# A two-layer hybrid decoder step: decay moved onto the keys of a chunked state scan, longer pauses, own buffers for small results, and another model for the scheduler

## The chip, the core and the metric

The kernel runs on one core of a Trainium2 chip. Its engines work side by side, each through its own queue of instructions in order: TensorE (PE, with its weight loads as PEld), VectorE (DVE), ScalarE (ACT), GpSimd (POOL) and SyncE (SP), which here issues transfers. The metric is the device time of one execution in microseconds (us). What is compared is the median of several executions.

## The reference

Two layers of a decoder take one step for a prompt of 512 tokens and 8 samples of 4 tokens each, 544 token columns in all. Weights are shared, states are per sample. The model width is 1024, in 32-bit floats. Cut to what matters here, one layer is:

```python
h = rmsnorm(x, p['norm1_g']) * (1 + mod[:, 1]) + mod[:, 0]
z = h @ p['w_in']
# four mixers on column ranges of z: pooling (yA), retention (yB), short convolution (yC), RWKV-7 (yD)
proj = jnp.einsum('btnc,ncd->btnd', branches, p['w_br'])
mixed = jnp.sum(gates * proj, axis=2) @ p['w_out']
x = x + mod[:, 2] * mixed
h2 = rmsnorm(x, p['norm2_g']) * (1 + mod[:, 4]) + mod[:, 3]
up, n_ffn = causal_dwconv(h2 @ p['w_up'], st_ffn, p['ffn_w'])
x = x + mod[:, 5] * (act @ p['w_down'])

def rwkv7_scan(r, w, k, v, a_vec, b_vec, S0):      # S: value x key, per head (4 heads of 64)
    def step(S, inp):
        rt, wt, kt, vt, at, bt = inp
        S = (S * wt[:, :, None, :]
             + jnp.einsum('bhij,bhj->bhi', S, at)[..., None] * bt[:, :, None, :]
             + vt[..., :, None] * kt[..., None, :])
        return S, jnp.einsum('bhij,bhj->bhi', S, rt)
```

The decay w is a vector over the key index, for each token. Retention (yB) has a fixed decay per head and a state that is carried from one 128-token chunk to the next. The result of RWKV-7 is normalised per head, gets a bonus term and is gated.

## The kernel before, in words

**The weight stream.** All large products have the tokens as moving columns, in two halves of 272, and a 128x128 piece of a weight matrix as the stationary operand. Each weight is split into a high and a low part: the high part is a cast on ScalarE (L113, `whi`), the low part a subtraction on VectorE (L114, `wlo`; GpSimd does it for two units at the start). Activations are split in the same way (L394 and L395). A product is then three matmuls, L133 to L135: high by high, high by low, low by high. There are 13248 of them, and `nmm` counts them as they are written. Weights come in units of 128x1024 (0.5 MB), loaded by SyncE some units ahead. Results go to one of three PSUM buffers `pd`.

**Side work.** The mixers, the adaptive scale and shift (`ada`) and the normalisations are generators. After each three stream matmuls `slot()` looks which generators are due and writes their next piece into the program. A generator ends a piece with `yield n`: it is due again after n more stream matmuls. So a pause is a length in stream matmuls, in multiples of three as things fall. The order of TensorE's instructions is the order in which this code writes them (`manual_schedule`). The order on VectorE, ScalarE, GpSimd and SyncE is chosen by the framework's scheduler, which simulates the program by a model of costs, and every wait between engines is put in by the framework.

**RWKV-7.** `rwkv` works through the prompt in 16 chunks of 32 tokens; a seventeenth stands for the samples. First `products(T)` makes, for four chunks at a time, keys and values that are scaled by the accumulated decays (`bkv`, L481; the left-hand side is written at L473 and L475), and `dec`, the whole decay of each chunk. TensorE transposes the keys (L500, result `psB`, copied to `BK`) and multiplies them with the left-hand side (L507, `psA`). Both have the accumulated decay divided out up to the chunk's end, so the state has to be multiplied by `dec` after each chunk. Then the scan runs, chunk by chunk: the matmuls of L653 (`psG`), copies of it to `gs` on ScalarE and VectorE (L615), the matmul L620 with the solved triangular system, copies of that into Z (L624), L673 (`psP`, what the chunk adds to the state) and L677 (output `pY`). Then the state is updated: `Pt = psP + Pn` (L685), two products of `Pt` with `dec` that go into Z for the next chunk (L691), and `Pn = Pt * dec` on GpSimd (L692). The pauses inside a chunk are `D_G` (behind L653), `D_S` (behind L620) and `D_P` (at the end). After the scan come the per-head normalisation (L383 sums on TensorE, Ln and Exp on ScalarE in L388 and L391, L771 to L775 on VectorE) and `yD`.

**Retention** runs per pair of heads. Transposes and scores are at L791 and L798; in the second piece are the chunk states (L819, summed into `Sb` by L825 and L827 on VectorE) and a copy for the samples (`vks`); in the third the outputs (L839 and, with `Sb`, L844). Its rope products wait for a transfer that exchanges rows (L1218), then GpSimd multiplies (L1220).

**Residual.** After the output projection, each block of 128 channels is added to x. For the second half of the tokens `residual` reads the PSUM buffer twice, for the prompt columns (L346) and for the 32 sample columns (L350, whose gates differ per sample), and adds the second to x in L353. L309 makes the next normalised activations from x.

**Buffers.** Most intermediate tiles, large or small, are taken in turn from one ring of ten buffers of 128x562 (`ZR`).

## Time and profile before

| | |
|---|---|
| median of 3 runs | 1978.6 us (1977.38 to 1979.33) |
| the profiled execution | 1977.9 us, span 1976.1 us, mean granted clock 0.990 |
| TensorE busy | 1908.5 us, 97% of the span |
| VectorE, ScalarE, GpSimd busy | 1111.4, 831.2, 315.7 us |
| PE idle, by the busy time | 67.6 us |
| first matmul of the weight stream | 30.85 us |
| HBM read | 213.33 MB, 113 GB/s over the span |

A row of the profile names line, engine, operation, and output and inputs by the program's names. In a timeline row, the first number is the start and the second the duration (us), and a bracket at its end gives the idle time of the engine before it with what released it. In a row of the table of groups, the count is followed by the total busy time, the mean in ns, and the idle time before them. `pd` and `pm` are PSUM tiles, `zr` tiles of the ring, `t` tiles of several kinds.

### The profile page before, as it was taken

How to read it: one execution, taken by the hardware profiler on the slowest of the kernel's cores; microseconds unless marked ns; L12 is line 12 of the kernel's file. 1: busy time of each engine (PE TensorE's matmuls, PEld its weight loads, DVE VectorE, ACT ScalarE, POOL GpSimd, SP SyncE). 2: the span in 40 equal slices, each digit the busy share in tenths (PEclk: the TensorE clock that was granted, in tenths of full speed). 3: DMA queues.
4: the chain of work that ended last, by engine and by line, in shares of the span. 5: the costliest groups of instructions: out<-in, count | busy, mean ns of one | idle time of the engine just before them, and what ended most of it. 6: DMA issues, size and time to landing. Idle time of an engine off the chain costs nothing.

```text
span 1976.1 us, 39220 instructions
## 1 busy us (share of the span) xinstructions
PE 1908.5 (97%) x16188; PEld 1829.6 (93%) x16188; DVE 1111.4 (56%) x2267; ACT 831.2 (42%) x1581; POOL 315.7 (16%) x627
## 2 busy tenths in 40 slices
PE   5999999999999999999999999999999999999997
PEld 4989888899999998899989899889999999999997
DVE  5466654643565653455673667556335765455565
ACT  4642332452445531435455433326424555243542
POOL 2120123213001210112201201232210012011210
PEclk8999999999999999999999999999999999999998
DMA  7323434423342257622332132124224222222231
GB/s 311 98 87 112 139 117 149 141 82 95 125 148 104 91 205 291 234 86 86 120 130 66 57 106 68 65 95 127 76 85 163 72 80 93 86 86 86 90 101 46
DMA packets 75555, 227.16 MB, mean 115 GB/s; under 512 B 20208, under 2 KB 23072, under 8 KB 73584
## 3 DMA queue, kind: packets, MB, share of 16 engines
q1 hardware_dynamic: 69872, 210.43, 31.9%
q0 software_dynamic: 3536, 11.53, 1.7%
q10 hardware_dynamic: 1968, 2.69, 0.5%
q8 instruction: 127, 2.08, 0.4%
q14 instruction: 52, 0.43, 0.1%
HBM read 213.33 MB, written 9.06 MB: 113 GB/s over the span
## 4 chain that ended last, share of the span: by engine, by line
PE 90%; DVE 5%; ACT 2%; DMA 1%; issue 1%; DVEq 0%; ACTq 0%
PE pd L133 27%; PE pd L135 26%; PE pd L134 26%; PE pm L236 2%; DVE wlo L114 1%; PE pm L673 1%; ACT whi L113 1%; DMA raw<-in_wst 1%; PE pm L500 1%; PE pm L677 1%; PE pm L653 0%; DMA t<-in_wada 0%; PE pm L507 0%; PE pm L620 0%; PE pm L383 0%
## 5 line engine op out<-in xcount | busy, mean ns | idle before, releaser
L133 PE MATMUL pd<-t,whi 128*128 128x272 f32 x4104 | 1207.3, 294 | 7.5 <-DVE zr L350 3.6
L135 PE MATMUL pd<-t,wlo 128*128 128x272 f32 x4104 | 1187.5, 289 | 0.0
L134 PE MATMUL pd<-t,whi 128*128 128x272 f32 x4104 | 1181.8, 288 | 0.1
L133 PEld LDWEIGHTS pd<-t,whi 128*128 128x128 f32 x4104 | 773.9, 189 | 39.9 <-issue 26.4
L134 PEld LDWEIGHTS pd<-t,whi 128*128 128x128 f32 x4104 | 775.7, 189 | 1.3 <-DVE t L395 0.3
L135 PEld LDWEIGHTS pd<-t,wlo 128*128 128x128 f32 x4104 | 774.3, 189 | 0.0
L114 DVE TENSOR_TENSOR wlo<-raw,whi 128x1024 fp32r<-128x1024 f32 x256 | 316.9, 1238 | 301.7 <-ACT whi L113 301.4
L113 ACT CAST whi<-raw 128x1024 fp32r<-128x1024 f32 x258 | 270.5, 1049 | 433.4 <-PE pd L134 419.6
L1276 POOL COPY off<-zr 128x18 f32<-128x18 f32 x88 | 76.2, 866 | 558.8 <-ACT zr L1274 558.8
L346 DVE SCALAR_TENSOR_TENSOR t<-pd,mod,t 128x272 f32<-128x272 f32 (+1 forms) x160 | 76.9, 481 | 112.5 <-PE pd L135 111.6
L1274 ACT COPY zr<-pd 128x272 f32<-128x272 f32 (+2 forms) x264 | 72.7, 311 | 78.4 <-PE pd L135 78.4
L1129 ACT ACTIVATE zr<-pd 128x272 f32<-128x272 f32 x128 | 50.3, 395 | 110.3 <-PE pd L135 106.2
L1111 DVE TENSOR_TENSOR zr<-pd,zr 128x272 f32<-128x272 f32 x96 | 41.1, 437 | 98.8 <-PE pd L135 98.1
L1113 POOL TENSOR_TENSOR t<-t,zr 128x272 f32<-128x272 f32 x64 | 71.3, 1133 | 112.5 <-DVE zr L1111 112.4
L1040 DVE SCALAR_TENSOR_TENSOR zr<-zr,par,zr 128x560 f32<-128x560 f32 x92 | 73.4, 800 | 10.0 <-ACT zr L1039 9.9
L1041 DVE SCALAR_TENSOR_TENSOR zr<-zr,par,zr 128x560 f32<-128x560 f32 x92 | 73.4, 801 | 2.8
L1039 ACT ACTIVATE zr<-zr,par 128x560 f32<-128x560 f32 x92 | 70.2, 765 | 6.8
L394 ACT CAST t<-zr 128x544 fp32r<-128x544 f32 (+1 forms) x96 | 49.5, 530 | 53.4 <-DVE zr L1287 53.0
L395 DVE TENSOR_TENSOR t<-zr,t 128x544 fp32r<-128x544 f32 (+1 forms) x96 | 54.5, 580 | 30.7 <-ACT t L394 30.4
L276 ACT ACTIVATE zr<-t 128x272 f32<-128x272 f32 (+1 forms) x72 | 32.2, 455 | 82.8 <-DVE t L346 54.6
L133 PE MATMUL pd<-t,t 128*128 128x272 f32 x224 | 64.8, 289 | 0.2
L134 PE MATMUL pd<-t,t 128*128 128x272 f32 x224 | 64.5, 288 | 0.0
(283 smaller groups left out, 1770.1 us busy)
## 6 DMA issues: line engine op xcount, KB each, us to landing
raw<-in_wst SPq DMA_DIRECT2D x276, 512.0 KB, 3.4
t<-in_wada SPq DMA_DIRECT2D x32, 1024.0 KB, 9.5
raw<-in_wada SPq DMA_DIRECT2D x24, 512.0 KB, 3.4
zr<-in_rope POOLq DMA_DIRECT2D x16, 272.0 KB, 3.6
t<-in_wada SPq DMA_DIRECT2D x8, 512.0 KB, 6.1
t<-in_xT SPq DMA_DIRECT2D x4, 544.0 KB, 6.1
zr<-zr ACTq DMA_DIRECT2D x32, 68.0 KB, 2.9
t<-in_xT SPq DMA_DIRECT2D x2, 1088.0 KB, 7.1
```

Of the source, the lines that this page charges most:

```text
L113: S.copy(hi, raw)
L114: (G if (l, u) in ((0, 1), (0, 2)) else V).tensor_tensor(out=lo, in0=raw, in1=hi, op=SUB)
L133: PE.matmul(ps, lhsT=a, rhs=xh, start=first, stop=False)
L134: PE.matmul(ps, lhsT=a, rhs=xl, start=False, stop=False)
L135: PE.matmul(ps, lhsT=b, rhs=xh, start=False, stop=last)
L346: V.scalar_tensor_tensor(out=x[:, c0:c0 + npc], in0=ps[:, :npc], scalar=gate[:, m, 0:1], in1=x[:, c0:c0 + npc], op0=MUL, op1=ADD)
L1039: S.activation(cv, u[:, 0:560], AF.Copy, scale=wcol(0))
L1040: V.scalar_tensor_tensor(out=cv, in0=u[:, 1:561], scalar=wcol(1), in1=cv, op0=MUL, op1=ADD)
L1041: V.scalar_tensor_tensor(out=cv, in0=u[:, 2:562], scalar=wcol(2), in1=cv, op0=MUL, op1=ADD)
L1113: (V if last else G).tensor_tensor(out=a[:, c0:c1], in0=a[:, c0:c1], in1=gs, op=ADD)
L1274: pad_evac(lambda o, i, sl: S.copy(o, i), u, ps, half, 2)
L1276: G.tensor_copy(off[:, 22 * s + j], u[:, 512:562].rearrange("p (x t) -> p x t", t=2)[:, 0:25:3, :])
```

## The change

Four things are changed.

1. The pauses: `D_G`, `D_S` and `D_P` go from 12, 12, 18 to 16, 16, 20, and the two pauses around the products from 48 and 44 to 60 and 56. Because pieces are written at multiples of three, the pause behind L653 goes from 12 to 18 stream matmuls, and so does the one behind L620; a whole chunk goes from 42 to 57, a step of the products from 45 to 57.
2. The keys carry the decay of their chunk: `bkd = bkv * dec` is a new product on VectorE for the 16 prompt chunks (four per layer and four chunks each), and the transposes take `bkd`. `psP` then comes out already multiplied, so the state is `Z = psP + E` with `E = Z * dec` of the chunk after. The additions are done on VectorE straight from PSUM into Z; `E` is made on GpSimd, in two halves.
3. Four kinds of small results (32 or 128 columns) get a ring of their own of five buffers, `ZS`.
4. The scheduler of the other engines is given the timeline simulator as its model (`schedule_with_timeline_sim=True`).

```diff
-D_G, D_S, D_P = 12, 12, 18
+D_G, D_S, D_P = 16, 16, 20
...
+    zsp = ctx.enter_context(tc.tile_pool(name="zsp", bufs=5))
...
+    def ZS(n):
+        return zsp.tile([128, n], F32, tag="zs", name=nm("zs"))
...
             if half == 1:
-                t = ZR(32)
+                t = ZS(32)
...
-            return bkv
+
+            bkd = ZR(512)
+            bkdv = bkd[:, 0:4 * n].rearrange("p (q c x) -> p q c x", q=2, x=64)
+            if T < 4:
+                V.tensor_tensor(out=bkdv, in0=bkv.rearrange("p q c w t -> p q c (w t)"),
+                                in1=dec[:, :, 4 * T:4 * T + nch].unsqueeze(3).broadcast_to([128, 2, nch, 64]), op=MUL)
+            return bkv, bkdv if T < 4 else bkv.rearrange("p q c w t -> p q c (w t)")
 
         bkn = products(0)
-        yield 48, True
+        yield 60, True
...
-                        PE.matmul(psB[kv_rows(q), cc:cc + 64], lhsT=bkv[r, p, c].rearrange("r w t -> r (w t)"),
+                        PE.matmul(psB[kv_rows(q), cc:cc + 64], lhsT=bkd[r, p, c],
...
-                yield 44, True
+                yield 56, True
...
-            pP = psP[:, 0:128].rearrange("r (p i) -> r p i", p=2)
-            db = dec[:, :, ch:ch + 1].broadcast_to([128, 2, 64])
-            Pt = M["pool"].tile([128, 2, 64], F32, tag="pt", name=nm("pt"), bufs=2)
-            if Pn is None:
-                V.tensor_copy(Pt, pP)
-            else:
-                V.tensor_tensor(out=Pt, in0=pP, in1=Pn, op=ADD)
-            Pn = M["pool"].tile([128, 2, 64], F32, tag="pn", name=nm("pn"), bufs=2)
             if ch < 15:
                 Zt, cn = (Z, 1) if c % 2 == 0 else (Zn, 0)
+                E = M["pool"].tile([128, 2, 64], F32, tag="pt", name=nm("pt"), bufs=2)
                 for q in range(2):
                     r = par_rows(q)
-                    V.tensor_tensor(out=Zt[q][r, cn], in0=Pt[r], in1=db[r], op=MUL)
-            G.tensor_tensor(out=Pn, in0=Pt, in1=db, op=MUL)
+                    pP = psP[r, 0:128].rearrange("r (p i) -> r p i", p=2)
+                    if ch:
+                        V.tensor_tensor(out=Zt[q][r, cn], in0=pP, in1=Eo[r], op=ADD)
+                    else:
+                        V.tensor_copy(Zt[q][r, cn], pP)
+                    G.tensor_tensor(out=E[r], in0=Zt[q][r, cn], in1=dec[r, :, ch + 1:ch + 2].broadcast_to([64, 2, 64]), op=MUL)
+                Eo = E
...
-                g0 = ZR(128)
+                g0 = ZS(128)
...
-        sms_s = ZR(32)
+        sms_s = ZS(32)
-        vks = ZR(128)
+        vks = ZS(128)
...
-    with tile.TileContext(nc) as tc:
+    with tile.TileContext(nc, schedule_with_timeline_sim=True) as tc:
```

How this moves instructions is shown at three places. Lines of the changed kernel are 4 higher up to some L485, and 10 or 11 higher behind it.

The residual on VectorE, in the first layer's output projection at the second half of the tokens, before. L346 and L350 read the PSUM tile `pd`, L114 is a weight split, L290 and L309 belong to the next normalisation:

```order
L346 SCALAR_TENSOR_TENSOR t_845_6216<-pd_6489,mod_94,t_845_6216 128x240
L114 TENSOR_TENSOR wlo_6629<-raw_6626,whi_6628 128x1024
L290 RECIPROCAL zr_6516<-zr_6516 128x272
L346 SCALAR_TENSOR_TENSOR t_845_6216<-pd_6530,mod_94,t_845_6216 128x240
L309 TENSOR_TENSOR zr_6519<-t_845_6216,zr_6516 128x272
L350 TENSOR_TENSOR zr_6525<-pd_6489,mod_94 128x32
```

The same place now (L350 is the former L346, L354 the former L350, L118 the former L114, L294 the former L290):

```order
L350 SCALAR_TENSOR_TENSOR t_834_6211<-pd_6484,mod_97,t_834_6211 128x240
L354 TENSOR_TENSOR zs_6520<-pd_6484,mod_97 128x32
L357 TENSOR_TENSOR t_834_6211<-t_834_6211,zs_6520 128x32
L118 TENSOR_TENSOR wlo_6624<-raw_6621,whi_6623 128x1024
L294 RECIPROCAL zr_6511<-zr_6511 128x272
L350 SCALAR_TENSOR_TENSOR t_834_6211<-pd_6525,mod_97,t_834_6211 128x240
L354 TENSOR_TENSOR zs_6571<-pd_6525,mod_97 128x32
```

Both readers of a `pd` tile stand one behind the other now, where four instructions stood between them.

The first products of the first layer on VectorE, now, up to the new product (L491); L446 and L447 prepare the keys, L477 and L479 the left-hand side, L485 is the former L481, and L1051 the former L1040:

```order
L446 SCALAR_TENSOR_TENSOR t_121_999<-t_121_999 128x544
L447 TENSOR_TENSOR t_72_615<-t_72_615,zr_1153 128x544
L477 TENSOR_TENSOR t_149_1163<-t_121_999,zr_1169 64x2x4x31
L477 TENSOR_TENSOR t_150_1164<-t_121_999,zr_1169 64x2x4x31
L479 TENSOR_TENSOR t_150_1164<-t_73_616,zr_1169 64x2x4x32
L118 TENSOR_TENSOR wlo_1205<-raw_1202,whi_1204 128x1024
L485 TENSOR_TENSOR zr_1179<-t_121_999,zr_1169 128x4x32
L485 TENSOR_TENSOR zr_1179<-t_72_615,zr_1169 128x4x32
L491 TENSOR_TENSOR zr_1184<-zr_1179,dec_596 128x512
L118 TENSOR_TENSOR wlo_1269<-raw_1266,whi_1268 128x1024
L1051 SCALAR_TENSOR_TENSOR zr_1198<-zr_1135,par_91,zr_1198 128x560
```

A weight split (L118) now stands ahead of the last two products of the keys, and the sum L1051, which stood ahead of them, stands behind.

The end of RWKV-7 and the first retention pair of the first layer on VectorE, now. L782 to L786 are the former L771 to L775, L836 and L838 the former L825 and L827 (`Sb`), L842 the former L831:

```order
L782 TENSOR_TENSOR t_73_616<-t_73_616,zr_4661 128x544
L833 TENSOR_TENSOR zs_4784<-pm_4767,cst 64x32
L200 SCALAR_TENSOR_TENSOR scl_99<-mod_97,par_91 128x72
L842 TENSOR_TENSOR zr_4794<-zs_4786,cst 64x512
L783 TENSOR_SCALAR t_73_616<-t_73_616,par_91 128x544
L836 COPY t_632_4686<-pm_4775 128x64
L782 TENSOR_TENSOR t_73_616<-t_73_616,zr_4662 128x544
L785 TENSOR_TENSOR t_73_616<-t_73_616,t_121_999 128x544
L838 TENSOR_TENSOR t_632_4686<-pm_4775,t_632_4686 128x64
L783 TENSOR_SCALAR t_73_616<-t_73_616,par_91 128x544
L786 TENSOR_TENSOR t_73_616<-t_73_616,t_121_999 128x544
L838 TENSOR_TENSOR t_632_4686<-pm_4775,t_632_4686 128x64
```

Before, L771 to L775 were all done ahead of the first scores of retention, and L825 to L827 stood behind them with one weight split and L831 in between. Now the two are threaded.

## The prediction

> **What bounds the kernel now.** I read the page's busy times and its chain first.

> ```profile
> PE 1908.5 (97%) x16188; PEld 1829.6 (93%) x16188; DVE 1111.4 (56%) x2267; ACT 831.2 (42%) x1581; POOL 315.7 (16%) x627
> PE 90%; DVE 5%; ACT 2%; DMA 1%; issue 1%; DVEq 0%; ACTq 0%
> ```

> TensorE is busy for 1908.5 of the 1976.1 us span, and the change takes no matmul from it. So only its 67.6 us of idle time can move, and each term must name a stall of PE that shrinks, goes or is born. PE's table of waits lists them as total us, times, longest.

> ```profile
> PE pm L287 <- DVE zr L279: 14.9, 3, 12.4
> PE pm L620 <- DVE gs L615: 10.4, 10, 1.3
> PE pm L500 <- DVE zr L481: 8.4, 3, 4.0
> PE pd L133 <- DVE zr L350: 8.2, 6, 2.8
> PE pd L133 <- DVE zr L1111: 2.5, 2, 1.2
> ```

> The first is the start, before any work. The other four lie at places which the change rearranges: 29.5 us, 1.5% of the span, and that caps what it can win there. The unit of length is the weight stream of L133 to L135, since the hand-written PE order counts its pauses in those matmuls. From PE's timeline:

> ```profile
> 1015.17 0.37 PE L133 MATMUL pd<-t,whi 128*128 128x272 f32 x1 [2.82 <-DVE zr L350]
> 1015.38 0.29 PE L134 MATMUL pd<-t,whi 128*128 128x272 f32 x1
> ...
> 1017.40 0.29 PE L135 MATMUL pd<-t,wlo 128*128 128x272 f32 x1
> 1018.44 0.36 PE L133 MATMUL pd<-t,whi 128*128 128x272 f32 x1 [0.75 <-DVE zr L350]
> ```

> From 1015.38 to 1017.40 lie 16 steps: 0.126 us per matmul. A pause longer by 6 matmuls gives whoever is waited for 0.75 us, at no cost to PE, since the stream must run anyway.

> **Residual, the wait on L350.** Two of the six waits stand in the rows above. VectorE in the same window:

> ```profile
> 1012.59 0.46 DVE L346 SCALAR_TENSOR_TENSOR t<-pd,mod,t 128x240 f32<-128x240 f32 x1
> 1012.97 0.43 DVE L309 TENSOR_TENSOR zr<-t,zr 128x272 f32<-128x272 f32 x1
> 1013.35 1.23 DVE L114 TENSOR_TENSOR wlo<-raw,whi 128x1024 fp32r<-128x1024 f32 x1
> 1014.49 0.43 DVE L309 TENSOR_TENSOR zr<-t,zr 128x272 f32<-128x272 f32 x1
> 1014.84 0.18 DVE L350 TENSOR_TENSOR zr<-pd,mod 128x32 f32<-128x32 f32 x1
> ```

> L346 and L350 both read one PSUM buffer; PE needs it back. L350 takes 0.18 us and needs nothing but that buffer and the gate, yet VectorE does two L309 and a weight split in between: L350 ends at 15.02, 1.9 us after L346 could hand over (12.59 + 0.46 = 13.05). In the changed order L350 stands directly behind its L346 in every such place. That takes away about 1.9 of the 2.82 us wait, and the rest only if L346 itself also comes earlier: ahead of it here stood another split, which moves back behind it. For the six, 8.2 us of idle plus some 0.08 us each for the restart (0.21 instead of 0.126 in the rows above) is at most 8.7. Bounds: 8.7 won if all go, 4 if only the delay behind L346 goes. I take **−7.5**.

> **Scan, the wait on L615.** Per chunk: L653, copies of its result on ScalarE and VectorE (L615), L620. Two chunks, uncontended and contended:

> ```profile
> 278.80 0.60 PE L653 MATMUL pm<-z,t 128*128 128x128 f32 x4
> 280.75 0.33 PE L620 MATMUL pm<-gs,t 128*128 128x64 f32 x2
> ...
> 245.50 0.85 DVE L1161 TENSOR_TENSOR t<-t 128x676 f32<-128x676 f32 x1
> 246.38 0.46 DVE L615 COPY gs<-pm 32x64 f32<-32x64 f32 x2
> 246.99 0.41 PE L620 MATMUL pm<-gs,t 128*128 128x64 f32 x2 [1.07 <-DVE gs L615]
> ```

> The uncontended round trip is 1.95 us, and 12 matmuls of pause are 1.5 us (the four short L653 fill part of the rest). The contended ones lie 1.0 us late on average (10.4 / 10), behind some other VectorE operation. The pause grows to 18 matmuls, +0.75 us: ten waits lose at most 0.75 each, 7.5. VectorE's part of the chunk changes little: the state update was one addition (L685), then two products with the decay (L691); now it is two additions straight from PSUM. The decay product goes to POOL, which did one operation (L692) and now does two:

> ```profile
> L691 DVE TENSOR_TENSOR z<-pt,dec 64x128 f32<-64x128 f32 x60 | 20.8, 347 | 1.6
> L692 POOL TENSOR_TENSOR pn<-pt,dec 128x128 f32<-128x128 f32 x32 | 15.3, 479 | 101.7 <-DVE pt L685 57.8 <-DVE pt L683 43.8
> ```

> Two of about 0.5 us are hidden by the chunk, now 57 matmuls or 7.1 us (42 before); if POOL is busy elsewhere the next chunk's state is late (rival (c)). I take **−6.5**; bounds −10.4 and −3.

> **Products, the wait on L500.** The first products of each layer, and the windows around them and around the residual stall above (busy us and instructions of PE, PEld, DVE, ACT, POOL; then the granted clock):

> ```profile
> 118.14 1.03 PE L500 MATMUL pm<-cst,zr 64*64 64x64 f32 x28 [3.62 <-DVE zr L481]
> ...
> 114.50:118.00 3.50, 0.02 (x2) 0.00 (x0) 3.46 (x8) 0.45 (x2) 3.43 (x6) 1.00 0.00 0
> 119.20:122.70 3.50, 3.50 (x44) 2.57 (x41) 3.42 (x9) 0.59 (x1) 1.88 (x2) 0.51 0.00 0
> 1015.00:1018.40 3.40, 2.52 (x18) 2.33 (x18) 3.26 (x12) 3.33 (x8) 0.00 (x0) 1.00 0.50 155
> ...
> L747 DVE TENSOR_TENSOR zr<-pm,zr 128x512 f32<-128x512 f32 x4 | 2.8, 692 | 0.9 <-PE pm L742 0.9
> ```

> VectorE is full there (3.46 of 3.50 us), so PE waits for its queue. The pause grows by 12 matmuls: 1.5 us. VectorE's queue ahead of the first L500 gains one weight split (1.23 as above), and the new product of keys and decay, 128x512. Nothing in the trace is this operation; nearest is L747, also 128x512 with two inputs, 0.69 us. One L1040 moves behind:

> ```profile
> L1040 DVE SCALAR_TENSOR_TENSOR zr<-zr,par,zr 128x560 f32<-128x560 f32 x92 | 73.4, 800 | 10.0 <-ACT zr L1039 9.9
> ```

> Net +1.23 + 0.69 − 0.80 = +1.1 us, so −0.4 per layer; in layer 1 (two waits, 4.8 us) no split comes in, so −1.2. The other products have VectorE time to spare: 57 matmuls are 7.1 us, and with the products' own short matmuls about 10, against 9 to 10 of VectorE work, tight. **−1.6**; from −5 (queue reordered better than I read it) to +4 (later products become late too: four per layer by 0.5).

> The windows show something else: after the 3.6 us idle the clock was 0.51 for 3.5 us, a further 1.7 us, and after 2.82 it stayed 1.00. My expected wait, 3.62 + 1.1 − 1.5 = 3.2, falls between the two. [...]

> **Project, the wait on L1111.** The evacuation stands in VectorE's queue behind L872, which waits 6.35 us for ScalarE's Exp (L391):

> ```profile
> 433.95 0.66 ACT L391 ACTIVATE zr<-zr 128x544 f32<-128x544 f32 x1
> 434.64 0.73 DVE L872 TENSOR_TENSOR t<-t,zr 128x544 f32<-128x544 f32 x1 [6.35 <-ACT zr L391]
> ```

> In the new order the evacuations come before it. **−2.5** (0 to −2.5).

> **A wait that the change adds.** With longer chunks the scan's normalisation ends next to the first retention pair: the last L383 stands at matmul 1863 before and 2169 now, and that pair's output matmuls (L839, L844) come 27 matmuls after it, 3.4 us, plus L383's own four and some 24 short ones, about 3 (an estimate). L844 needs the running sums Sb (L825, L827). VectorE's new order threads these between the steps of the normalisation, which wait for ScalarE:

> ```profile
> 365.51 1.86 ACT L388 ACTIVATE zr<-pm,eps 128x272 f32<-128x272 f32 x4 [0.29 <-PE pm L383]
> 368.43 1.28 ACT L391 ACT_TABLE_LOAD   x1
> 369.72 1.21 ACT L391 ACTIVATE zr<-zr 128x544 f32<-128x544 f32 x2
> 370.41 1.36 DVE L771 TENSOR_TENSOR t<-t,zr 128x544 f32<-128x544 f32 x2 [1.15 <-ACT zr L391]
> 371.69 1.03 DVE L772 TENSOR_SCALAR t<-t,par 128x544 f32<-128x544 f32 x2
> ...
> L827 DVE TENSOR_TENSOR t<-pm,t x12: 208/214/226, 384.8 to 1393.5; 128x64 f32<-128x64 f32 x12
> ```

> ScalarE now does Ln ×3, table, Exp, table, Ln, table, Exp (a table load more on each side): from L383, 0.4 + 3 × 0.47 + 1.28 + 0.6 + 1.28 + 0.47 + 0.2 (a copy) + 1.28 + 0.6 = 7.5 us. Then VectorE: L771 and L774 (0.68 each), L827 (0.2), L772 (0.5), L774's twin (0.68), L827: the third sum is there at about 10.3, and PE wants it at about 6.4. Per layer a stall of up to 3.9; none if PE comes later than I count. Two layers: **+6**, from 0 to +11 (with a stretch of half clock behind each). The normalised result itself is first read at matmul 2256 as before, 87 matmuls (11 us), two stages of retention and that stall after L383, some 25 us, where the chain needs about 17 (13 in the rows before, 365.5 to 378.4, plus the table loads and sums between): 0, with 8 us of cover.

> **Start.** Behind the same adaptive matmuls, PE's first weight matmul is at 30.85.

> ```profile
> 30.85 0.60 PE L133 MATMUL pd<-t,whi 128*128 128x272 f32 x1
> ...
> 20.96 3.61 POOL L114 TENSOR_TENSOR wlo<-raw,whi 128x1024 fp32r<-128x1024 f32 x1 [6.24 <-ACT whi L113]
> ...
> 22.38 2.49 DVE L942 TENSOR_TENSOR t<-t,zr 128x272 f32<-128x272 f32 x1
> ```

> The new order puts all but two L942 and the first split ahead of the first scale (L196), and so ahead of ScalarE's L297 of chunk 0. One of these operations took 2.49 us, where L309 with the same shape takes 0.43, while POOL split weights. I work out L297 at 28 to 29, and the first weight matmul at 32.4; ScalarE's copies for the next chunks come earlier, which gives some back. **+1.5** (−1 to +3). [...]

> The own buffers for small results take some writers out of the ring of ten, and by themselves remove no wait that PE's table names: 0.

> **Sum.** −7.5 − 6.5 − 1.6 − 2.5 + 6 + 1.5 = −10.6 us, against the profiled 1977.9 (span 1976.1 and 1.8 around it). The median of the runs is 1978.6, 0.7 above; there the sum is **1968**.

> **Rivals.** (a) *All waits go and none is born.* PE reaches L844 later than I count, the retention sums are in time, and VectorE, idle for 44% of the span, takes the rest. −8.7 − 9 − 5 − 2.5 + 0 = −25: 1953. Against it: the third sum's 10.3 us is a chain of ScalarE steps, not a matter of load.
> (b) *The gains come back elsewhere.* The new order of three engines creates waits that I did not find, each of 1 to 3 us as the old ones are; four of 2 us take back 8: 1976. For it: the old order, made with the same freedom, left the last three rows of PE's table. Against it: none shows in the new order where I followed it.
> (c) *Slower: POOL's queue.* POOL now makes the decay product that the next chunk's state needs, and in the new order two of them per layer stand behind rope products, which wait for transfers:

> ```profile
> L1220 POOL TENSOR_TENSOR zr<-zr,zr 128x544 f32<-128x544 f32 x8 | 13.7, 1717 | 52.8 <-DMA zr<-zr 46.8 <-ACT zr L388 5.9
> ```

> That is 46.8 / 7 = 6.7 us of wait on average (it begins when POOL has nothing else, so it is no delay in itself). I count 5 to 8 us of slack, of the chunk's 7.1 and the wait before. Four products, each late by over 2.7 us, eat the whole gain; each late by 5 gives −10.6 + 20 = +9: 1988. Against it: before, the decay product stood at POOL too and its waits were for DVE only.

> **Chances.** The forecast (1960 to 1974) 0.60; (a), below 1960, 0.13; (b), 1974 to 1982, 0.16; (c), above, 0.11. The range that leaves 2 in 10 out is 1955 to 1980. About 0.2% is what a measurement tells from no change, 4 us: below 1974.6 is faster: 0.75; within 0.13; above 1982.6 slower: 0.12.

> **What would show it.** Right: PE's table of waits has no L350 and no L1111 row over 1 us, L620 under 5, L500 5.5 to 8, and a new row of 2 to 8 us for the retention sums at L844 (now L855). Wrong: an L844 row of nothing (then (a)), a row of PE waiting for POOL's decay product or its state (then (c)), or a first weight matmul before 30 or after 34. The forecast fails above all if the residual gain is undone: there VectorE has little room, and an evacuation standing behind a split again costs a wait of 1 to 3 us.

## The result, and the profile after

The change makes the kernel slower: 1990.49 us (median of 6, 1987.07 to 1996.49) against 1979.41 before (median of 6), a ratio of 1.006 with a 95% interval of 1.0044 to 1.0077. The forecast was 1968, and 1980 the end of its range.

The page of the changed kernel, its span and busy times:

```profile
span 1987.9 us, 39257 instructions
...
PE 1916.1 (96%) x16188; PEld 1837.4 (92%) x16188; DVE 1099.3 (55%) x2245; ACT 837.2 (42%) x1585; POOL 330.0 (17%) x655
```

The span grew by 11.8 us. TensorE's idle time grew by 4.2 (71.8 against 67.6), and its *busy* time by 7.6, with the same number of matmuls: some of them ran slower. PE's table of waits (total us, times, longest):

```profile
PE pm L291 <- DVE zr L283: 15.6, 3, 12.8
PE pd L137 <- ACT t L398: 9.6, 2, 9.1
PE pm L510 <- DVE zr L491: 7.6, 2, 3.8
PE pd L137 <- DVE zr L1122: 6.3, 6, 1.9
PE pd L138 <- DVE t L399: 5.7, 3, 2.6
PE pm L855 <- DVE t L838: 4.9, 4, 1.7
PE pd L137 <- DVE t L1122: 4.7, 5, 1.6
PE pm L630 <- DVE gs L625: 4.5, 6, 2.6
```

Set beside the table of before: the scan's wait (L620, now L630) fell from 10.4 to 4.5; the products' (L500, now L510) from 8.4 to 7.6; the residual's (L350, 8.2) is gone. New are 4.9 for the retention sums (L855, once L844), as forecast. Not forecast are 11.0 us for the projection's evacuations (L1122 with its two outputs, once L1111 with 2.5) and 5.7 for the low parts of the normalised activations (L399). The wait for L398 is the start, where before L212 waited 9.0 for L209.

The clock is the other half. Behind two stalls of the changed kernel (columns as in the windows shown before the result; `PEclk`, the granted clock of TensorE, is the number ahead of the last two):

```profile
416.30:423.00 6.70, 6.70 (x28) 5.47 (x25) 2.87 (x5) 4.48 (x6) 1.47 (x3) 0.50 0.26 86
450.40:453.70 3.30, 3.30 (x17) 3.30 (x16) 1.58 (x3) 0.54 (x2) 2.20 (x2) 0.50 0.50 159
453.80:457.10 3.30, 3.30 (x29) 3.30 (x28) 0.00 (x0) 0.40 (x1) 0.00 (x0) 1.00 0.00 0
```

In a window of 3.3 us the stream does 17 matmuls at half clock and 29 at full. The stream's step in one such stretch, from its first to its last row, 16 steps in 3.62 us, 0.226 us each and not 0.126:

```profile
418.83 0.43 PE L139 MATMUL pd<-t,wlo 128*128 128x272 f32 x1
...
422.45 0.43 PE L137 MATMUL pd<-t,whi 128*128 128x272 f32 x1
```

Summing all start-to-start times of PE by kind gives where the span went. "Half clock" is the time above 0.126 us of stream steps in such stretches, "waits" that of single steps over 0.6 us, "short" the rest above 0.126; "side work" is all time between stream matmuls that have other matmuls between them, with the waits there.

| us | start | half clock | waits in the stream | short | side work | sum against before |
|---|---|---|---|---|---|---|
| before | 30.9 | 5.0 | 13.7 | 23.9 | 224.8 | |
| changed kernel | 32.1 | 13.5 | 20.1 | 24.1 | 220.4 | +11.8 |
| model alone | 32.2 | 5.7 | 19.8 | 27.7 | 229.8 | +16.8 |
| pauses alone | 31.4 | 11.1 | 15.1 | 25.0 | 228.8 | +13.0 |
| own buffers alone | 31.5 | 4.4 | 7.9 | 23.2 | 222.1 | −9.3 |
| all but the model | 31.2 | 9.2 | 11.2 | 24.4 | 228.8 | +6.4 |
| the same, retention later | 31.3 | 2.8 | 7.5 | 25.8 | 217.3 | −13.6 |
| changed kernel, retention later | 32.0 | 7.9 | 20.6 | 23.9 | 214.2 | +0.2 |

Each row is one profiled execution; that of the last kernel was the shortest of its runs (1978.11 to 1986.98). The side work did get 4.4 us shorter. The stream's own waits grew by 6.4, and half clock took 8.5 more. The runs below tell which part of the change does this.

### The profile page after: what moved, and what is told of

It reads as the page before. It is cut to its first block, busy times and chain, and to the rows that moved or that the text cites. A ratio compares the mean times of both kernels' runs of the same rounds, so it can differ in the third digit from the quotient of the medians.

```text
span 1987.9 us, 39257 instructions
## 1 busy us (share of the span) xinstructions
PE 1916.1 (96%) x16188; PEld 1837.4 (92%) x16188; DVE 1099.3 (55%) x2245; ACT 837.2 (42%) x1585; POOL 330.0 (17%) x655
## 3 DMA queue, kind: packets, MB, share of 16 engines
q10 hardware_dynamic: 1968, 2.69, 0.5%
## 4 chain that ended last, share of the span: by engine, by line
PE 87%; DVE 5%; ACT 3%; DMA 2%; issue 2%; SPq 0%; ACTq 0%; DVEq 0%; POOL 0%; POOLq 0%
PE pd L137 27%; PE pd L139 26%; PE pd L138 26%; PE pm L240 2%; DVE wlo L118 1%; DMA raw<-in_wst 1%; PE pm L663 1%; PE pm L683 1%; DVE z L617 1%; PE pm L687 1%; DMA t<-in_xinit 0%; DMA t<-in_wada 0%; PE pm L510 0%; DVE t L953 0%; PE pm L517 0%
## 5 line engine op out<-in xcount | busy, mean ns | idle before, releaser
L118 DVE TENSOR_TENSOR wlo<-raw,whi 128x1024 fp32r<-128x1024 f32 x256 | 315.3, 1232 | 318.6 <-ACT whi L117 318.0
L350 DVE SCALAR_TENSOR_TENSOR t<-pd,mod,t 128x272 f32<-128x272 f32 (+1 forms) x160 | 76.5, 479 | 115.2 <-PE pd L139 115.0
L1122 DVE TENSOR_TENSOR zr<-pd,zr 128x272 f32<-128x272 f32 x96 | 40.5, 435 | 90.3 <-PE pd L139 89.9
L1051 DVE SCALAR_TENSOR_TENSOR zr<-zr,par,zr 128x560 f32<-128x560 f32 x92 | 73.4, 801 | 6.6 <-ACT zr L1050 6.6
L399 DVE TENSOR_TENSOR t<-zr,t 128x544 fp32r<-128x544 f32 (+1 forms) x96 | 54.2, 578 | 29.2 <-ACT t L398 29.2
L398 ACT CAST t<-zr 128x544 fp32r<-128x544 f32 (+1 forms) x96 | 48.8, 530 | 47.7 <-DVE zr L1298 46.7
```

Of the source, the lines that this page charges most:

```text
L118: (G if (l, u) in ((0, 1), (0, 2)) else V).tensor_tensor(out=lo, in0=raw, in1=hi, op=SUB)
L350: V.scalar_tensor_tensor(out=x[:, c0:c0 + npc], in0=ps[:, :npc], scalar=gate[:, m, 0:1], in1=x[:, c0:c0 + npc], op0=MUL, op1=ADD)
L1051: V.scalar_tensor_tensor(out=cv, in0=u[:, 1:561], scalar=wcol(1), in1=cv, op0=MUL, op1=ADD)
```

## The experiments

**The model alone, all but the model, the pauses alone, the buffers alone.** Of the first kernel the edit to the kernel before is

```diff
-    with tile.TileContext(nc) as tc:
+    with tile.TileContext(nc, schedule_with_timeline_sim=True) as tc:
```

> The kernel before, with nothing changed but the scheduler's model. Theory 'order': the new order on VectorE, ScalarE and GpSimd is what costs. The waits on the projection's evacuation (11.0 us in the changed kernel, 2.5 before) and on the split of the normalised activations (5.7, 0 before) belong to it, and with them more half clock (54.5 us of the span in the changed kernel, 30.7 before). Then this kernel takes 1987 to 1995 us, with both rows in PE's table of waits. Theory 'pauses': the longer pauses push RWKV-7 into the retention and the gates, and the order is neutral. Then this kernel takes 1977 to 1982 us.

Measured: 1993.84 us, ratio 1.0069 (1.0053 to 1.0084). The new order costs by itself. The new waits of the changed kernel are there, in other sizes. In PE's table of this kernel, behind the start, the scan (9.4) and the products (9.8):

```profile
PE pd L133 <- DVE zr L350: 5.5, 7, 2.2
PE pd L133 <- ACT zr L1129: 4.6, 2, 2.3
PE pd L134 <- DVE t L395: 3.2, 2, 1.7
PE pd L133 <- DVE t L1111: 3.1, 3, 1.4
```

The expected extra half clock is not: 5.7 us of it in the stream, as before (5.0). So "order" holds for the waits and the time, and these waits did not bring more half clock. Also, L350's wait shrinks to 5.5 but stays: this model does not remove it.

The second kernel is the changed one with that line as it was.

> The changed kernel with the scheduler's former model; pauses, keys with decay and own buffers stay. Theory 'order': 1965 to 1973 us, with no wait over 1 us on the projection's evacuation, the wait of L620 at about 4 and the residual's at 0. Theory 'pauses': 1985 us or more, with the evacuation's waits still there.

Measured: 1985.51 us, 1.0026 (1.0016 to 1.0036). By its stated range this is "pauses", at the lower edge: 5 us better than the whole change, yet 12 worse than "order" allowed, and waits for evacuations are still there, 5.7 us of the 11.0. Its table of waits, behind the two rows of the start:

```profile
PE pm L510 <- DVE zr L491: 8.4, 2, 4.8
PE pm L830 <- ACT t L803: 6.1, 2, 3.1
PE pm L630 <- DVE gs L625: 4.8, 7, 2.0
PE pd L137 <- DVE zr L1122: 3.9, 3, 1.6
PE pm L855 <- DVE t L838: 1.8, 1, 1.8
```

The wait on L803 is new: the second retention pair's transposed keys. The third kernel:

```diff
-D_G, D_S, D_P = 12, 12, 18
+D_G, D_S, D_P = 16, 16, 20
...
-        yield 48, True
+        yield 60, True
...
-                yield 44, True
+                yield 56, True
```

> The kernel before with the longer pauses alone (16, 16, 20, and 60 and 56 around the products). Theory 'order': the scan's wait falls from 10.4 to about 4 and the retention sums add up to 5, so 1974 to 1980 us. Theory 'pauses': 1985 to 1992 us.

Measured: 1992.14 us, 1.0065 (1.0048 to 1.0082): "pauses", at the upper end of its range. The scan's wait fell only to 6.9, the products' to 5.4. New are 6.1 for the keys (L819 on L792), 1.8 for the sums (L844), 2.1 for the state (L653 on L691), and 6 us of half clock. The fourth kernel has only `zsp`, `ZS` and its four users, as in the diff.

> The kernel before with the own buffers for the small results alone. The built order already has L350 right behind L346, so the buffers and not the model should take the residual's wait away: 8.2 us of PE idle go, and the time is 1969 to 1973 us. Were the model needed for it (as the prediction had it, with the buffers at 0), the wait would stay and the time be 1978 to 1981 us.

Measured: 1968.09 us, 0.994 (0.9926 to 0.9955). The first rows of its table are

```profile
PE pm L291 <- DVE zr L283: 16.9, 3, 13.0
PE pm L624 <- DVE gs L619: 10.7, 10, 1.2
...
PE pm L504 <- DVE zr L485: 8.3, 3, 4.0
PE pd L137 <- DVE zr L1115: 2.5, 2, 1.2
```

with no row of the residual. The buffers take that wait away, not the model. The likely way is that the scheduler placed a 32-column result late because it had to wait for its turn in the ring of ten, and the PSUM buffer was kept until then; which of the four small results matters was not tried apart. Of the 12 us, 8.2 are the residual's wait; the rest was not traced.

So two parts cost some 13 us each, and one wins 12.

**The keys alone.** The decay on the keys and the new state update, with the old pauses, ring and model (the diff's parts with `bkd`, `E` and `Pn`).

> The kernel before with the decay on the keys and the new state update alone (old pauses, one ring of buffers, old model). By addition: the pauses alone gave +12.2 us, the own buffers alone -11.9, and the two with this part and the old model +5.6, so this part should give about +5: 1983 to 1987 us. If it is free, as the prediction had it within its cover, 1977 to 1982 us, and the +5 is an interaction of the other two.

Measured: 1979.40 us, 0.9999 (0.9989 to 1.0008). In time the part is free. Its table is not: the products' wait rose from 8.4 to 11.4 and the scan's from 10.4 to 12.2, while half clock in the stream fell by some 3 us in the profiled execution. The addition failed by 5: the pauses and the rest interact.

**Filling the wait for the sums.** In the changed kernel, with `psC` allocated earlier:

```diff
         for T in range(1, 4):
+            for _ in range((0, 0, 4, 2)[T]):
+                PE.matmul(psC[:, 0:HALF], lhsT=ones, rhs=cst[:, 0:HALF], start=True, stop=True)
             for q in range(2):
```

> The changed kernel with six more matmuls per retention pair (128x272, some 0.39 us each), whose result nobody reads: four between the outputs with the first and the second sum, two before the third, just where PE waits 1.7 and 0.8 us. Theory 'clock': half the loss behind a wait is the half clock that follows it; with PE kept busy the two stretches of 6.8 us at half clock (at 416 and 1396 us in the changed kernel) go, and the time falls by 4 to 7 us to 1983 to 1987, though work was added. Theory 'idle': only the waits themselves count; the matmuls take the place of the waits where there is one and add some 2 us in the two pairs that have none: 1990 to 1995 us.

Measured: 1991.96 us, 1.0063 (1.0048 to 1.0078), as the changed kernel. The clock record has no half clock left at those two places, half clock in the stream fell by 3.9 us (13.5 to 9.6), and the wait for the sums from 4.9 and 0.4 to 0.3. But the side work grew by 7.4 us. The 24 added matmuls are two instructions each in the trace and took 12.6 us from start to start, where some 9 were meant; less the 5 us of waits, that is the whole growth. The stretches that are left lie at other places than before (554 and 1333 us among them), and the profiled execution was the slowest of five (1996.99). The time is the one that "idle" named and goes against "clock" as I had stated it, but the filler cost more than the half clock that it took away, so the test does not settle what that half clock costs; shown is only that the stretches at the two places went when the filler came.

**Retention later.** In the changed kernel:

```diff
-        while not (M.get("ret0") and M.get("scan_done")):
+        while not (M.get("ret0") and M.get("rwkv_done")):
```

> The changed kernel with the first retention pair started when RWKV-7's tail has been written, not when its scan has: its pieces stand 48 stream matmuls later (scores at 2196 and not 2148, outputs at 2244 and not 2196). Theory 'crowd': the longer pauses cost because the end of the scan now meets retention. Then the waits for the retention sums (5.3 us) go, with the half clock behind them: 1980 to 1986 us. If the sums' wait only moves to the second pair or to the gates, no change, 1988 to 1993 us.

Measured: 1983.32 us, 1.0011 (1.0002 to 1.002): 7 less by the medians, as "crowd" says. In its table the row of the sums is gone, the L399 row is 5.8 and L1122's two 4.8 and 3.9. The crowd is real; the model's waits stay.

**Shorter lengthenings, on the own buffers alone.** First, only the products' pauses, 60 and 56.

> Own buffers alone (1968.1 us) plus the longer pauses around the products (60 and 56), with the scan's pauses as before. In the run with all the pauses the products' part was 1.5 us faster in layer 0 and 3.3 in layer 1, and the loss came behind, in scan and retention. Theory 'crowd': the products' gain stays, 1962 to 1966 us, as the scan ends only some 60 matmuls later. If any lengthening ahead of retention costs, 1968 us or more.

Measured: 1977.33 us, 0.9985 (0.9976 to 0.9994), 9 us lost against 1968.1. Position by position along the stream, the products won 2 us by matmul 900 and the scan and retention behind lost it again, 2.4 us in layer 0 and 8 in layer 1. The old scan ended (last L383) at 1863 and the first pair began at 1944; now the end is at 1923. By the stated ranges "crowd" as I had put it is wrong, and any lengthening costs. What may save it is a nearer limit than I had set: RWKV-7's tail, 13 us long, has to be nearly over when the pair begins. That is an inference; of the 8 us in layer 1 the table shows only a wait of 1.4 us at the pair's first piece. Then a shift by 6, which leaves 75 matmuls between (1869 and 1944):

```diff
-        yield 48, True
+        yield 54, True
```

> Own buffers alone (1968.1 us), with the first pause ahead of the products 54 and not 48: all products and scan steps stand 6 stream matmuls later, nothing else changes in length. Theory 'alignment': what a step meets on VectorE (a weight split, an evacuation) depends on where it stands in the stream, and the old places were better than most; then 1971 to 1978 us, with other chunks among the scan's waits. Theory 'length': only a late end of the scan costs; 6 matmuls are nothing to that, and the first products' wait falls by up to 0.75 us per layer: 1966 to 1968.5 us.

Measured: 1971.11 us, 0.9954 (0.9939 to 0.9968); by its median at the lower edge of "alignment", but the interval overlaps that of the own buffers alone, and the two profiled executions agree (1968.19 and 1968.32). The shift is nearly harmless. And 15 for `D_G`:

> Own buffers alone (1968.1 us), with the pause behind L653 15 and not 12, the chunk 45 matmuls and not 42, the scan's end 51 matmuls later (1914 and not 1863), still 30 ahead of the first retention pair, which stays at 1944. Theory 'length': the scan's wait falls by 0.38 us in each of ten places, nothing meets retention, 1964 to 1967 us. Theory 'alignment': 1969 to 1976 us, the scan's wait no smaller than its 10.7.

Measured: 1981.31 us, 1.001 (0.9999 to 1.0021), 13 lost. From its table:

```profile
PE pm L657 <- DVE z L695: 7.3, 7, 3.2
PE pm L818 <- DVE zs L826: 3.5, 2, 2.2
...
PE pm L624 <- DVE gs L619: 2.0, 4, 0.6
```

"Length" was right on the scan's wait (10.7 to 2.0) and wrong on the time: the next step of the chunk (L657 on the state update L695) now waits 7.3, one of them 3.2, and retention's second piece 3.5. The time lies above both ranges. Two things go together here, and no run separates them: other places in the stream meet other VectorE work, and the tail (1914) meets the pair at 1944. Half clock in the stream grew as well, by 6.6 us against the own buffers alone.

**All but the model, retention later.**

> The whole change with the old model and with the first retention pair started behind RWKV-7's tail. With the new model the later start took 7 us off; with the old one the change took 1985.5. Theory 'crowd': the waits of L819 for the transposed keys (6.1 us) and for the sums (1.8) go, 1976 to 1980 us, still not under the own buffers alone (1968.1), as the scan's own waits and alignment stay. If only the new model's order suffered from the crowd, 1984 to 1987 us.

Measured: 1963.22 us (1962.95 to 1964.26), 0.9917 (0.9903 to 0.9932): 22 us under the same kernel with retention early (1985.51), and the fastest of all, 13 us under the range of "crowd" and 5 under the own buffers alone, which I had ruled out. Rows of its table:

```profile
PE pm L510 <- DVE zr L491: 8.4, 2, 4.8
PE pm L630 <- DVE gs L625: 4.9, 7, 2.1
PE pd L137 <- DVE t L1122: 1.8, 3, 0.8
PE pd L137 <- DVE zr L1122: 1.6, 1, 1.6
```

No row for keys or sums. Along the stream the 20 us between the two profiled executions nearly all fall between matmuls 2100 and 2400 and between 8700 and 9000, ten in each layer, at the end of RWKV-7. More than the waits (6.1 + 1.8) went: half clock fell from 9.2 to 2.8 us in the stream, and the rest of the gain lies in the side work, where half clock counts too. What the crowd does shows on ScalarE at the second pair of layer 0, in the kernel with the pauses alone, where PE waits for the same copies (6.1 us in both):

```profile
427.25 1.28 ACT L391 ACT_TABLE_LOAD   x1
428.54 0.66 ACT L391 ACTIVATE zr<-zr 128x544 f32<-128x544 f32 x1
431.43 1.05 ACT L113 CAST whi<-raw 128x1024 fp32r<-128x1024 f32 x1 [2.23 <-PE pd L134]
...
434.62 1.07 ACT L792 COPY t<-pm 128x512 f32<-128x512 f32 x2
```

ScalarE stands still for 2.2 us ahead of a weight cast that waits for PE, while the copies that PE will wait for (L792) are behind the cast in ScalarE's queue:

```profile
435.74 0.72 PE L819 MATMUL pm<-t 128*64 128x64 f32 x16 [3.06 <-ACT t L792]
```

With retention later, or in the kernel before, PE does not wait for these copies at all. Not run: the own buffers with the old pauses and retention later, so how much of the 5 us under the own buffers alone is owed to the longer pauses is open.

**Four PSUM buffers for the stream.** In the changed kernel:

```diff
-    psd = ctx.enter_context(tc.tile_pool(name="psd", bufs=3, space=bass.MemoryType.PSUM))
-    psm = ctx.enter_context(tc.tile_pool(name="psm", bufs=5, space=bass.MemoryType.PSUM))
+    psd = ctx.enter_context(tc.tile_pool(name="psd", bufs=4, space=bass.MemoryType.PSUM))
+    psm = ctx.enter_context(tc.tile_pool(name="psm", bufs=4, space=bass.MemoryType.PSUM))
```

> The changed kernel with four PSUM buffers for the weight stream and four for the rest (three and five before). PE waits 11.0 us for evacuations of the projection (L1122). Theory 'depth': an evacuation is late by 0.5 to 2 us, and a fourth buffer (8 to 24 more matmuls of distance, 1 us at least) covers most of it: these waits fall under 3 us, with two or three stretches of half clock, 1978 to 1984 us, unless the side work now waits for its own buffers. Theory 'order': VectorE's queue is late by whole operations, so the waits move to the next unit: 1988 to 1994 us.

Measured: 1985.62 us, 1.0031 (1.0014 to 1.0047). The waits behaved as "depth" says:

```profile
PE pd L138 <- DVE t L399: 8.1, 5, 2.5
...
PE pm L1195 <- DVE z L634: 1.9, 1, 1.9
...
PE pd L137 <- DVE t L1122: 0.4, 1, 0.4
```

11.0 us of evacuation waits became 0.4. The time fell by 5 and stays above the 1984 of "depth", and the intervals touch: L399 rose from 5.7 to 8.1, the side work waits 1.9 at a new place, and half clock in the stream rose to 15.0.

## Why the prediction was wrong

Put in the order of the forecast's sum, its terms measure −8.2 − 5.9 − 0.8 + 8.5 + 5.3 + 1.3 = +0.2 us, where −10.6 was forecast. Nearly the whole difference is one term, the projection. The rest of the loss is in two things that the sum did not have: the split of the activations (+5.7) and half clock (+8.5 in the stream).

**The projection, −2.5 forecast, +8.5 measured.** This step failed first. I read in the new order that evacuations come before the retention's products, and they do not where it counts:

```profile
447.80 0.73 DVE L883 TENSOR_TENSOR t<-t,zr 128x544 f32<-128x544 f32 x1 [7.16 <-ACT zr L395]
448.56 0.72 DVE L884 TENSOR_TENSOR t<-t,t 128x544 f32<-128x544 f32 x1
449.20 0.43 DVE L1122 TENSOR_TENSOR zr<-pd,zr 128x272 f32<-128x272 f32 x1
...
449.69 0.39 PE L137 MATMUL pd<-t,whi 128*128 128x272 f32 x1 [1.92 <-DVE zr L1122]
```

VectorE waits 7.2 us for Exp, and the evacuation now stands behind both products (L872 and L873 of before), not behind one. The same wait, 1.92 us again, comes in layer 1 at 1430 us. These two are 3.8 of the 11.0 us. The others over 0.5 us lie at the earlier gates, at 181, 222, 322, 1169, 1209 and 1306 us, which I had not followed, since nothing waited there before. There the evacuation stands behind other side work on VectorE: at 222 and 1209 us, for example, behind ten and fifteen copies of L617 (2.0 and 3.0 us). Neither part makes the 11.0 by itself: it is 5.0 with the model alone, 3.3 with the pauses alone and 5.7 with all but the model.

**The split of the activations, 0 forecast, +5.7.** Also not followed. At the second half of the normalisation:

```profile
1030.02 1.21 DVE L118 TENSOR_TENSOR t<-raw,t 128x1024 fp32r<-128x1024 f32 x1
1031.15 0.18 DVE L357 TENSOR_TENSOR t<-t,zs 128x32 f32<-128x32 f32 x1
1031.25 0.78 DVE L399 TENSOR_TENSOR t<-zr,t 128x272 fp32r<-128x272 f32 x2
...
1031.73 0.59 PE L138 MATMUL pd<-t,whi 128*128 128x272 f32 x1 [2.62 <-DVE t L399]
```

A weight split that nobody needs yet, of a unit five units later in the stream, stands ahead of the low part that the next matmul needs. With the old model this wait is 0.2 us at most, with the new one it is 3.2 to 8.1 in all five kernels that ran it. So it belongs to the model.

**Half clock, 0 forecast beyond what there was, +8.5 in the stream.** I saw it only at the first products and as a tail of the sums' wait. Of the ten new stalls of 1 to 3 us, six have 3.4 or 6.8 us at 0.50 beside or behind them, and four have none. In these single executions it comes above all with the pauses (11.1 in the pauses alone, 5.7 in the model alone), and starting retention later takes 5.6 away with the new model and 6.4 with the old. How much of the time it costs beyond these sums is open, since the filler was too dear to tell.

**Own buffers, 0 forecast, −12 us measured.** The residual's term itself was right (−7.5, 8.2 of idle gone), but I gave it to the scheduler's order. The order was a consequence of the buffers. Of the 12 us only some 4 are beyond the residual's term. Had I built the kernel with the buffers alone and read its order, I would have seen it.

**The wait that the change adds, +6 forecast: right in mechanism, too small in reach.** PE waited 5.3 us for the sums. VectorE's row of the decisive sum:

```profile
411.75 0.72 DVE L782 TENSOR_TENSOR t<-t,zr 128x544 f32<-128x544 f32 x1 [0.62 <-ACT zr L395]
412.39 0.72 DVE L785 TENSOR_TENSOR t<-t,t 128x544 f32<-128x544 f32 x1
413.02 0.22 DVE L838 TENSOR_TENSOR t<-pm,t 128x64 f32<-128x64 f32 x1
...
413.30 0.43 PE L855 MATMUL pm<-t,t 64*64 64x128 f32 x4 [1.68 <-DVE t L838]
```

But the price of the crowd is not this wait: starting retention later is worth 22 us with the old model (1985.51 to 1963.22) and 7 with the new one.

**Scan, products, start, keys: right in size.** −6.5 forecast and −5.9 measured; −1.6 and −0.8; +1.5 and +1.3; and the keys free (0.9999). In the products the size hides a wrong part: the longer pauses alone took 3.0 us off this wait, as counted, but the decay on the keys alone put 3.0 on, not 2 × 0.69, and the new order took off the last 0.8. At the first products of layer 0 the wait was 3.79 us in the changed kernel, not 3.2, and the clock fell to 0.50 for 3.4 us (122.7 to 126.1 us) as before (119.2 to 122.7), so the sum rightly had no gain of clock there. The scan's gain exists in the changed kernel; it is paid back behind it.

**The rivals.** (c), POOL's decay product behind a rope product, did not occur: no row of PE's or VectorE's waits names the decay product. By its time the result lies in the band of (c). What came is (b), waits that I had not found, with more than twice its price. I gave it 16%, reasoning that none showed where I had followed the order; but I had followed it where PE had waited before, which says nothing on the places where it had not. Of the signs that were to show the forecast wrong by another road (no wait at L844, a wait for POOL, a start before 30 or after 34 us) none came; the one that failed is the row of the evacuations, which was to stay at or under 1 us.

By parts, each alone, the change is: model +13.9, pauses +12.2, buffers −11.9, keys −1.1 (differences to the median of before of the same job); their sum is +13.1, against 11.1 measured for the whole. That the two agree is chance: the last three add up to −0.8 and give +5.6 together, and the model then adds some 5 and not 13.9. Why the new model's order costs 20 us once the crowd is gone (1983.32 against 1963.22) is shown only in part: 14.5 us of waits at L1122 and L399 against 3.6 in the fastest kernel, and 5.1 us more half clock in the stream. How the model comes to that order was not tried.

## What to carry to other kernels

When a chain of side work is slowed on purpose, look at what its *end* now meets, not only at the waits along it. A few pauses of 6 matmuls won 6 us in the scan and lost 20 where the tail met the next chain, and one condition (start the next one when the tail is done) turned a loss into the fastest version, with the old model. A new model for a scheduler is a change of every queue, so it is tried by itself; and small results that share a ring with large ones can go with a late release of a buffer that the main stream needs.

## What was not expected of the hardware

In these profiles the length of one wait does not tell whether half clock follows. After 2.82 us of idle time the clock stayed at 1.00 in the kernel before (window 1015.00 to 1018.40 of the prediction), while the same wait was followed by 0.50 in the pauses alone (from 1023.4 us). After 1.92 us it fell to 0.50 in layer 0 of the changed kernel (450.40 to 453.70), and after the same 1.92 us in layer 1 (1430 us) it did not.

```profile
446.94:450.35 3.41, 1.49 (x12) 1.27 (x11) 2.52 (x4) 3.37 (x6) 0.63 (x1) 1.00 0.00 0
1426.57:1429.98 3.41, 1.56 (x13) 1.34 (x11) 1.79 (x4) 3.38 (x4) 0.00 (x0) 1.00 0.00 0
...
1019.94:1023.35 3.41, 0.59 (x5) 0.40 (x4) 3.37 (x9) 3.17 (x6) 0.00 (x0) 1.00 0.45 154
...
1010.13:1013.54 3.41, 2.22 (x18) 2.00 (x17) 3.41 (x7) 1.47 (x3) 0.00 (x0) 1.00 0.30 107
1013.54:1016.95 3.41, 1.78 (x14) 1.81 (x15) 3.41 (x10) 3.35 (x9) 0.00 (x0) 1.00 0.75 253
```

Half clock follows the first window (44% busy) and the third (17%), not the second (46%), nor the last two (65% and 52%), between which the wait of 2.82 us is divided. Over the profiled executions of the kernel before and of the changed kernel, behind their first 100 us, half clock followed each of the 7 full-clock windows in which TensorE was busy for less than 45%, 4 of 11 windows between 45% and 60%, and 3 of 1062 above that. So the busy time in the window before does not settle it either: two of the three were busy throughout (330.9 and 1307.1 us in the kernel before).

The stretches also differ between kernels whose first stage is written alike: some 14 us of half clock at the start of the kernel before (20.3 to 33.9 us, at 0.50) are absent in the fastest one.
